# Attention as one stream of block steps over all head pairs, with the normalising on ScalarE

## The chip, the core and the metric

The kernel runs on one core of a Trainium2 chip. A core has TensorE (PE in the profile; its weight loads stand apart as PEld), VectorE (DVE), ScalarE (ACT), GpSimd (POOL), and SyncE (SP), which here only issues transfers. Each engine works through its own list of instructions in order. The metric is device microseconds of one execution.

## The reference

One inference step of a two-layer network on 640 tokens (512 latent, 128 context) of width 1024. Both layers are half FFN, mixer, half FFN. The mixer of layer 0 is a Fourier transform, that of layer 1 is attention, and only that attention is touched here. Cut to it:

```python
q, k, v = split(h @ w_qkv)                        # 16 heads of 64
# context queries (128): all context keys
p = softmax(q k^T);  o = p v
# latent queries (512 = 8 rows x 64 columns): 8 x 16 neighbours with a bias, and 128 cached keys
p = softmax(concat(q k_win^T + bias, q k_cache^T));  o = p_loc v_win + p_ctx v_cache
y = o @ w_out
```

## The kernel before

Activations lie transposed, channels on partitions and tokens along the row, in two halves of 320 tokens. Projections are made with split operands: each weight and each activation is a high part and a low part, and `mm3` (L206) makes one product of three matmuls (L209 to L211). Weights come as units of 128x1024. `send` (L166) loads a unit into one of four `raw` buffers, ScalarE writes its high part (L192) and VectorE its low part (L194) into one of six slots.

Attention (`attention`, L890) works by head pair: channel block c of eight holds heads 2c and 2c+1. `qk(c)` projects queries and keys of a pair, 96 matmuls, and writes them in two parts (L909 to L940); `double` (L950) copies the keys to the other 64 partitions. `v_tiles` projects values for two pairs at once, five token tiles of 24 matmuls each.

The attention of one pair is five blocks: four of 128 latent queries with 384 keys, and one, "c", for the context queries. A block has three pieces for each head. **Scores**: two matmuls into PSUM (L1041), VectorE adds the bias, writes `left` and takes the maximum (L1045), negates it (L1028), ScalarE takes the exponential and its sum (L1029), VectorE takes the reciprocal (L1030) and multiplies `left` by it (L1031). **Turn**: three transposes on TensorE (L1055), and ScalarE copies the result out of PSUM into `right` (L1057). **Values**: products with v, `right` as the moving operand, accumulated in the PSUM bank `sum` (L1070); the two heads write 64 PSUM partitions each. There are four `left` buffers, three `right` buffers, two `score` banks, and one each of `turn` and `sum`. In step n of a pair stand the scores of block n, the values of block n-2, and the turns of block n-1; after five steps two more empty the pipeline.

What sets the order: `weave` (L879) takes the list of a pair's pieces and a length in ns, and `tick` drops a piece into the projections each time that an assumed amount of matmul time has passed. So the pieces of pair c lie between the projections of pair c+1. `flush` emits what is left, and `behind` (L197) emits jobs of the next modulation: one job loads 128x1024 weights into a `raw` buffer and has VectorE make two dot products of them (L349). A scheduler then orders each engine's list by priority and readiness of its own; the pieces are what it is given, the list is what it makes.

Pairs 0 to 6 run under the projections of the next pair. Pair 7 runs under the first seven eighths of the first four output projections (`out_proj`, L749), whose input is `y`, split into two parts (L203, L204).

Of the kernel before, what the change touches and what calls it, by code (L numbers as in the profile page):

```python
# [15 lines left out]
ALU = mybir.AluOpType  # L16
PSUM = bass.MemoryType.PSUM

P = 128
# [50 lines left out]
for _c in range(2, NCH):  # L70
    QKV_ORDER += [("q", _c), ("k", _c)]
    if _c % 2 == 0 and _c > 2:
        QKV_ORDER += [("v0", _c // 2), ("v1", _c // 2)]
# [37 lines left out]
class Kernel:  # L111
# [778 lines left out]
    def attention(self, base, boundary):  # L890
# [70 lines left out]

        def v_tiles(quad, ts, at=at, bank="main"):
# [4 lines left out]
            for t in ts:  # L967
# [6 lines left out]
                for i, v in enumerate(values[quad]):  # L974
                    nc.vector.tensor_copy(v[:, t, :], ps[:, i * P : (i + 1) * P])
                    if t == 4:
                        nc.sync.dma_start(out=io["v_out"][2 * quad + i], in_=v[:, t, :])

        for half in (0, 1):
            self.finish(half)  # L980
            if half == 0:
                for c in (0, 1):
                    open_pair(c)
                    cached(c)
            pss = self.multi([self.unit(base + i) for i in range(4)], half)
            for i, ps in enumerate(pss):
                with self.tc.high_priority():
                    (query, key)[i % 2](i // 2, half, ps)
            if half:
                double(0)  # L990
                double(1)
            for quad in (1, 0) if half == 0 else (0,):
                while half == 0 and not self.normed[1][1 - quad]:
                    self.step(1)
                v_tiles(quad, ((0, 1), (2, 3, 4))[half], at if half else early, "score")
        qk_ns, v_ns = 4 * 8 * 3 * 147.0, 5 * 8 * 3 * 118.0
# [10 lines left out]
        parts = self.pair_parts(NCH - 1, pairs[NCH - 1], ctx_qk[NCH - 1], values[3][1])  # L1007
        for c in range(NCH - 1):
            for half in (0, 1):
                self.split(self.h.at(0, c, half), self.h.at(1, c, half), self.pair(self.y, c, half, 1))  # L1010
        self.weave(parts, 8000)
        def rest():
            self.flush()
            for half in (0, 1):
                self.split(self.h.at(0, NCH - 1, half), self.h.at(1, NCH - 1, half), self.pair(self.y, NCH - 1, half, 1))
        self.out_proj(1, base + len(QKV_ORDER), boundary, rest)

    def pair_parts(self, c, pair, qk, v):
# [3 lines left out]
        ks = pair[1:]  # L1022
        cache_v = self.cache[1][:, c * P : (c + 1) * P]
        state = {}

        def softmax(L, mx, w):
            sm = self.col(1)
            nc.vector.tensor_scalar_mul(mx, mx, -1.0)  # L1028
            nc.scalar.activation(L[:, :w], state["in"], AF.Exp, bias=mx, accum_out=sm)  # L1029
            nc.vector.reciprocal(sm, sm)  # L1030
            nc.vector.tensor_scalar_mul(L[:, :w], L[:, :w], sm)  # L1031

        def scores(p0, b):
# [5 lines left out]
            q = queries(pair, p0)[:, b * P : (b + 1) * P]  # L1039
            for part in range(2):  # L1040
                nc.tensor.matmul(o, q, tiles(ks[p0])[:, 5 * part : 5 * part + 5][:, BLOCK_KEYS[b]],  # L1041
                                 start=part == 0, stop=part == 1)
# [3 lines left out]
                                           scale=1.0, scalar=-3e38, op0=ALU.add, op1=ALU.max, accum_out=mx)  # L1046
            state["in"] = L
            softmax(L, mx, 384)
            state[p0, b] = L

        def turn(which, w):
            L = state.pop(which)
# [5 lines left out]
            state["t", which] = ptb  # L1058

        def values(b):  # L1060

            ptb = [state.pop(("t", (p0, b))) for p0 in range(2)]
# [3 lines left out]
            for at, q0, nq, tiles in taken:  # L1066
                for n, (i, k) in enumerate(tiles):
                    for p0 in range(2):
                        ds = slice(64 * p0, 64 * p0 + 64)
                        nc.tensor.matmul(state["o"][ds, q0 : q0 + nq], cache_v[:, ds] if k is None else v[:, k, ds],  # L1070
# [7 lines left out]
        def ctx_scores(p0):  # L1078
            ps = self.bank("score")
            nc.tensor.matmul(ps[:, :P], qk[:, p0 * P : (p0 + 1) * P], qk[:, 2 * P :], start=True, stop=True)  # L1080
            L = self.temp("left")
            mx = self.col(1)
            nc.vector.tensor_reduce(out=mx, in_=ps[:, :P], axis=mybir.AxisListType.X, op=ALU.max)
            state["in"] = ps[:, :P]
            softmax(L, mx, P)
            state[p0, "c"] = L

        blocks = [0, 1, 2, 3, "c"]
        both = lambda do: [partial(do, p0) for p0 in range(2)]
        parts = []  # L1090
        for n in range(len(blocks) + 2):
            if n < len(blocks):
                b = blocks[n]
# [150 lines left out]
```

## Time and profile before

| | us |
|---|---|
| median of three runs (2374.76 to 2378.6) | 2376.35 |
| the profiled execution | 2376.43 |
| its span, first to last instruction | 2374.6 |
| attention with its projections, 1571 to 1871 of the span | 300 |
| ... up to the first scores, to 1622 | 51 |
| ... pairs 0 to 5, to 1808 | 186 |
| ... pair 6, to 1844 | 36 |
| ... pair 7, to 1871 | 27 |

The borders are those of the copies that end a pair (L1076), rounded. In a profile, "PE sum L1070 <- ACT right L1057" means that the matmul of L1070 into `sum` stood idle until the ScalarE instruction of L1057 that wrote `right` had ended. TensorE is pipelined: the interval from one matmul's start to the next one's start is what a matmul costs, not its duration.

### The profile page before, as it was taken

Reading aid. Unit: us, or ns where it says so; the run is one execution under the profiler, and the core shown is the slowest. Engines: PE = TensorE matmul, PEld = TensorE weight load, DVE = VectorE, ACT = ScalarE, POOL = GpSimd, SP = SyncE. Lnnn points to the kernel's source line nnn. Section 1 sums busy time; section 2 is a strip of 40 time slices with the busy share of each in tenths; the row PEclk is TensorE's granted clock in tenths of the full one; section 3 lists DMA queues with packets and bytes.
Section 4 is the critical chain, followed back from the end, with each engine's and each line's share of the span. In section 5 each row is a group of like instructions: output and inputs, shape, how many; then the busy total and the mean of one; then the engine's idle time right before and its main releaser. Section 6 shows DMA issues by size and latency. Waiting matters only on the chain.

```text
span 2374.6 us, 39530 instructions
## 1 busy us (share of the span) xinstructions
PE 2302.0 (97%) x15692; PEld 2249.1 (95%) x15692; DVE 1743.5 (73%) x3112; ACT 1277.0 (54%) x2444; POOL 48.8 (2%) x50
## 2 busy tenths in 40 slices
PE   6899999998999999999999999999999999999997
PEld 5899999998999999999999999988888899999997
DVE  7788888389788878846878887368888585755553
ACT  3445545564564545547545555555556574545545
POOL 3200000000000000000000000000000000000000
PEclk9999999999999999999999999999999999999999
DMA  7134334333424433442234434223444222321241
GB/s 264 58 125 143 119 129 135 132 102 124 151 72 143 148 119 109 140 160 91 94 118 134 143 116 149 100 72 121 132 137 129 81 97 72 98 85 58 89 134 45
DMA packets 80142, 277.10 MB, mean 117 GB/s; under 512 B 8786, under 2 KB 15186, under 8 KB 79956
## 3 DMA queue, kind: packets, MB, share of 16 engines
q1 hardware_dynamic: 79684, 274.25, 35.5%
q8 instruction: 123, 2.02, 0.3%
q14 instruction: 63, 0.52, 0.1%
q10 hardware_dynamic: 272, 0.33, 0.0%
HBM read 263.00 MB, written 11.53 MB: 116 GB/s over the span
## 4 chain that ended last, share of the span: by engine, by line
PE 87%; DVE 5%; ACT 4%; issue 2%; DMA 1%; POOL 0%; SPq 0%; ACTq 0%; DVEq 0%
PE main L209 25%; PE main L211 25%; PE main L210 25%; PE score L209 2%; PE score L210 2%; PE score L211 2%; PE sum L1070 2%; DVE junk L349 1%; ACT hi L192 1%; PE turn L1055 1%; PE score L1041 1%; DVE lo L194 1%; PE sum L432 1%; DVE ring L204 1%; ACT right L1057 1%
## 5 line engine op out<-in xcount | busy, mean ns | idle before, releaser
L209 PE MATMUL main<-ring,hi 128*128 128x320 f32 x3872 | 1200.2, 311 | 19.5 <-ACT ring L203 18.1
L211 PE MATMUL main<-ring,lo 128*128 128x320 f32 x3872 | 1203.0, 311 | 2.9 <-POOL lo L194 2.9
L210 PE MATMUL main<-ring,hi 128*128 128x320 f32 x3872 | 1203.8, 311 | 1.6 <-DVE ring L204 1.5
L209 PEld LDWEIGHTS main<-ring,hi 128*128 128x128 f32 x3872 | 728.5, 188 | 25.5 <-ACT ring L203 20.3
L210 PEld LDWEIGHTS main<-ring,hi 128*128 128x128 f32 x3872 | 730.4, 189 | 5.2 <-DVE ring L204 3.1
L211 PEld LDWEIGHTS main<-ring,lo 128*128 128x128 f32 x3872 | 730.5, 189 | 5.0 <-POOL lo L194 3.4
L192 ACT ACTIVATE hi<-raw 128x1024 fp32r<-128x1024 f32 (+1 forms) x358 | 350.7, 982 | 480.9 <-PE main L210 385.4
L194 DVE TENSOR_TENSOR lo<-raw,hi 128x1024 fp32r<-128x1024 f32 (+1 forms) x354 | 398.3, 1125 | 167.9 <-ACT hi L192 166.7
L349 DVE SCALAR_TENSOR_TENSOR junk<-raw,wide 128x1024 bf16<-128x1024 f32 x256 | 312.4, 1220 | 12.8 <-DMA raw<-in_w_mod_t 10.1
L644 ACT ACTIVATE y<-main 128x320 f32<-128x320 f32 x320 | 138.3, 433 | 175.1 <-PE main L211 173.9
L385 DVE TENSOR_TENSOR total<-total,square 128x640 f32<-128x640 f32 x71 | 58.3, 823 | 115.8 <-ACT square L384 114.9
L632 ACT ACTIVATE main<-y 128x320 f32<-128x320 f32 x256 | 111.7, 439 | 23.5 <-DVE left L618 9.9
L210 PE MATMUL score<-ring,hi 128*128 128x320 f32 x384 | 118.7, 309 | 0.4 <-DVE ring L204 0.4
L209 PE MATMUL score<-ring,hi 128*128 128x320 f32 x384 | 118.9, 310 | 0.0
L211 PE MATMUL score<-ring,lo 128*128 128x320 f32 x384 | 118.6, 309 | 0.0
L194 DVE TENSOR_TENSOR lo<-sums,hi 128x1024 fp32r<-128x1024 f32 x64 | 78.2, 1222 | 54.0 <-ACT hi L192 54.0
L211 PE MATMUL main<-ring,ring 128*128 128x320 f32 x352 | 109.7, 312 | 5.8 <-POOL ring L194 5.8
L209 PE MATMUL main<-ring,ring 128*128 128x320 f32 x352 | 111.2, 317 | 0.0
L210 PE MATMUL main<-ring,ring 128*128 128x320 f32 x352 | 109.4, 311 | 0.0
L192 ACT ACTIVATE hi<-sums 128x1024 fp32r<-128x1024 f32 x64 | 67.9, 1060 | 27.3 <-PE main L210 20.5
L203 ACT ACTIVATE ring<-right 128x320 fp32r<-128x320 f32 x112 | 51.6, 469 | 45.6 <-DVE right L531 37.1
L604 DVE TENSOR_TENSOR left<-left,main 128x320 f32<-128x320 f32 x64 | 31.2, 487 | 59.6 <-PE main L211 59.6
(189 smaller groups left out, 2803.2 us busy)
## 6 DMA issues: line engine op xcount, KB each, us to landing
raw<-in_w SPq DMA_DIRECT2D x264, 512.0 KB, 3.6
raw<-in_w_mod_t SPq DMA_DIRECT2D x128, 512.0 KB, 3.7
raw<-in_qkv SPq DMA_DIRECT2D x26, 512.0 KB, 3.6
spill<-ring SPq DMA_DIRECT2D x12, 640.0 KB, 3.4
ring<-spill SPq DMA_DIRECT2D x12, 640.0 KB, 4.7
raw<-in_bias SPq DMA_DIRECT2D x16, 448.0 KB, 3.4
first<-in_w_mod_t SPq DMA_DIRECT2D x8, 512.0 KB, 10.2
raw<-in_four_in SPq DMA_DIRECT2D x8, 512.0 KB, 3.5
```

Of the source, the lines that this page charges most:

```text
L192: nc.scalar.activation(hi, raw[:, at], AF.Copy)
L194: engine.tensor_tensor(lo, raw[:, at], hi.bitcast(F32), op=ALU.subtract)
L203: self.nc.scalar.activation(hi, src, AF.Copy)
L209: mm(out, whi, xhi, start=start, stop=False)
L210: mm(out, whi, xlo, start=False, stop=False)
L211: self.latest = mm(out, wlo, xhi, start=False, stop=stop)
L349: last = self.nc.vector.scalar_tensor_tensor(out=self.junk, in0=raw, scalar=1.0, in1=self.wide[:, cond, :], op0=ALU.mult, op1=ALU.mult, ac ...
L385: nc.vector.tensor_tensor(acc, acc, sq, op=ALU.add)
L604: tt(a, q, z, op=ALU.subtract)
L632: nc.scalar.activation(ps[:, :HALF], self.y[:, m, lo:hi], AF.Copy)
L644: nc.scalar.activation(self.y[:, m, lo:hi], ps[:, :HALF], AF.Copy)
L1070: nc.tensor.matmul(state["o"][ds, q0 : q0 + nq], cache_v[:, ds] if k is None else v[:, k, ds], ptb[p0][:, i * P + at : i * P + at + nq], s ...
```

## The change

All forty blocks of the eight pairs become one list of steps (`attend` in place of `pair_parts`), so the pipeline is not emptied between pairs: step n holds the scores of block n, the values of block n-2 and the turns of block n-1 over the border of a pair. Five steps are woven into the projections of the next pair. The projections of values are spread over more pairs, two or three token tiles at a time; those of the second half of pair 1's queries and keys move behind the first scores. The multiplication by the reciprocal moves from VectorE to ScalarE (`scale`), ahead of the values of the block before. The negation of the maximum is folded into the scores' reduction (scale -1, minimum) and the exponential (scale -1); for "c" it stays. `behind` emits one modulation job in a step instead of three or four at the end of a pair. The split of `y` for pair 6 moves into the last steps.

```diff
-        for half in (0, 1):
-            self.finish(half)
...
-            pss = self.multi([self.unit(base + i) for i in range(4)], half)
...
-        for c in range(NCH - 1):
-            v_next = {0: 1, 3: 2, 5: 3}.get(c)
-            self.weave(self.pair_parts(c, pairs[c], ctx_qk[c], values[c // 2][c % 2]),
-                       (qk_ns if c else 0) + (v_ns if v_next else 0) - (0 if c else v_ns * 0.4))
-            if c:
-                qk(c + 1)
-            if v_next:
-                v_tiles(v_next, range(5) if c else (2, 3, 4))
-            self.flush()
-            self.behind(3 + (c < 3))
+        steps = self.attend(pairs, ctx_qk, values)
+        period = lambda c: [part for step in steps[5 * c : 5 * c + 5] for part in step]
+        qk_ns, v_ns = 4 * 8 * 3 * 147.0, 8 * 3 * 118.0
+        self.finish(0)
...
+        products([("q", 0), ("k", 0), ("q", 1), ("k", 1)], 0)
...
+        self.finish(1)
+        products([("q", 0), ("k", 0), ("v", 0, 3), ("v", 0, 4)], 1)
+        double(0)
+        v_tiles(0, (2,), early, "score")
+        plan = {0: (1, (2, 3, 4)), 2: (2, (0, 1)), 3: (2, (2, 3, 4)), 4: (3, (0, 1)), 5: (3, (2, 3, 4))}
+        for c in range(NCH - 1):
+            quad, ts = plan.get(c, (0, ()))
+            self.weave(period(c), (qk_ns if c else qk_ns / 2) + len(ts) * v_ns)
...
-        self.weave(parts, 8000)
+        steps[5 * NCH - 4].append(partial(parts_of, NCH - 2))
+        self.weave([part for step in steps[5 * NCH - 5 :] for part in step], 9000)
...
-            nc.vector.tensor_scalar_mul(mx, mx, -1.0)
-            nc.scalar.activation(L[:, :w], state["in"], AF.Exp, bias=mx, accum_out=sm)
+            nc.scalar.activation(L[:, :w], src, AF.Exp, bias=mx, scale=sign, accum_out=sm)
             nc.vector.reciprocal(sm, sm)
-            nc.vector.tensor_scalar_mul(L[:, :w], L[:, :w], sm)
...
+        def scale(c, b):
+            for p0 in range(2):
+                L, sm, w = state[c, b, p0]
+                nc.scalar.activation(L[:, :w], L[:, :w], AF.Copy, scale=sm)
...
+        blocks = [(c, b) for c in range(NCH) for b in (0, 1, 2, 3, "c")]
+        steps = []
         for n in range(len(blocks) + 2):
+            parts = []
             if n < len(blocks):
-                b = blocks[n]
-                parts += both(ctx_scores if b == "c" else lambda p0, b=b: scores(p0, b))
-            if n >= 2:
-                parts.append(partial(values, blocks[n - 2]))
-            if 1 <= n <= len(blocks):
-                b = blocks[n - 1]
-                parts += both(lambda p0, b=b: turn((p0, b), P if b == "c" else 384))
-        return parts
+                c, b = blocks[n]
+                parts += [partial(ctx_scores if b == "c" else scores, c, b, p0) for p0 in range(2)]
+            before = partial(scale, *blocks[n - 1]) if 1 <= n <= len(blocks) else None
+            after = partial(take, *blocks[n - 2]) if n >= 2 else None
+            parts.append(lambda both=(before, after): [do() for do in both if do])
+            if before:
+                parts += [partial(turn, *blocks[n - 1], p0) for p0 in range(2)]
+            if n < 35 and (n % 5 < 3 or n in (3, 8, 13)):
+                parts.append(self.behind)
+            steps.append(parts)
```

How the lists move. First place: TensorE in pair 6, block steps. `score`, `turn` and `sum` are PSUM banks, `main` rows are projections. Before, from a score on:

```order
L1041 MATMUL score_18967<-ring_18381,ring_18379 128x384 x2
L1055 MATMUL turn_18981<-ident,left_18923 128x128 x3
L210 MATMUL main_19000<-ring_15818,hi_18521 128x320
L211 MATMUL main_19000<-ring_15817,lo_18522 128x320
L209 MATMUL main_19098<-ring_15737,hi_18653 128x320
L210 MATMUL main_19098<-ring_15738,hi_18653 128x320
L211 MATMUL main_19098<-ring_15737,lo_18654 128x320
L1070 MATMUL sum_19035<-right_18985,square_18649 64x64
L209 MATMUL main_19098<-ring_15737,hi_18653 128x320
```

and in the change, from the turn of a block's second head on (the row after the last is the first of the six values that use this turn):

```order
L1103 MATMUL turn_19046<-ident,left_18933 128x128 x3
L209 MATMUL main_19016<-ring_15792,hi_18551 128x320
L210 MATMUL main_19016<-ring_15793,hi_18551 128x320
L211 MATMUL main_19016<-ring_15792,lo_18552 128x320
L1077 MATMUL score_19066<-ring_18543,ring_18542 128x384 x2
L209 MATMUL main_19016<-ring_15817,hi_18551 128x320
L210 MATMUL main_19016<-ring_15818,hi_18551 128x320
L211 MATMUL main_19016<-ring_15817,lo_18552 128x320
L1077 MATMUL score_19078<-ring_18544,ring_18542 128x384 x2
L209 MATMUL main_19016<-ring_15817,hi_18551 128x320
L210 MATMUL main_19016<-ring_15818,hi_18551 128x320
L211 MATMUL main_19016<-ring_15817,lo_18552 128x320
```

Before, one value matmul follows the turn that feeds it after five projections, alone, and the other rows of its block come later as a second group; in the change nine projections and two scores lie between, and the values of a block stand together. From the first score to the last value, TensorE's list enters a group of values 79 times before (41 of these groups are one row) and 55 times in the change (15 of one row); the number of rows is the same, 224.

Second place: TensorE at the end of pair 7. Before, 39 rows of scores, turns and values follow the last projection of the stretch, among them:

```order
L1055 MATMUL turn_19490<-ident,left_19407 128x128 x3
L1080 MATMUL score_19508<-rms_19083 128x128
L1080 MATMUL score_19521<-rms_19083 128x128
L1055 MATMUL turn_19499<-ident,left_19418 128x128 x3
L1070 MATMUL sum_19429<-right_19494,ring_15811 64x128
L1070 MATMUL sum_19429<-right_19503,ring_15811 64x128
```

In the change projections reach in between the two turns of the last latent block:

```order
L1103 MATMUL turn_19480<-ident,left_19404 128x128 x3
L209 MATMUL main_19259<-ring_15817,hi_19012 128x320
L210 MATMUL main_19259<-ring_15818,hi_19012 128x320
L211 MATMUL main_19259<-ring_15817,lo_19013 128x320
L209 MATMUL main_19282<-ring_15817,hi_19220 128x320
L210 MATMUL main_19282<-ring_15818,hi_19220 128x320
L211 MATMUL main_19282<-ring_15817,lo_19221 128x320
L1103 MATMUL turn_19489<-ident,left_19416 128x128 x3
L1119 MATMUL sum_19374<-right_19484,square_18261 64x128
```

From the turn of the second head on, eleven rows of turns and values stay behind the last projection.

Third place: ScalarE in the change, while the blocks of pair 4 run. `hi` is the high part of a weight unit, `ring` from `main` the high part of keys:

```order
L192 ACTIVATE hi_18264<-raw_18262 128x1024
L1105 ACTIVATE right_18128<-turn_18124 128x384
L1097 ACTIVATE left_18071<-left_18071,col_18074 128x384
L1063 ACTIVATE left_18146,col_18149<-left_18146,col_18147 128x384
L936 ACTIVATE ring_17955<-main_18117 64x128
L936 ACTIVATE ring_17956<-main_18117 64x128
L936 ACTIVATE ring_17955<-main_18117 64x192
L936 ACTIVATE ring_17956<-main_18117 64x192
L1063 ACTIVATE left_18161,col_18164<-left_18161,col_18162 128x384
L192 ACTIVATE hi_18270<-raw_18268 128x1024
L1105 ACTIVATE right_18200<-turn_18196 128x384
L1097 ACTIVATE left_18146<-left_18146,col_18149 128x384
```

The scaling (L1097) of a block is a new row in this list, between exponentials (L1063), copies of turns (L1105) and splits. Outside the attention the lists of all engines are the same as before, row for row.

More of the change, by code (lines that the diff above doesn't have):

```diff
@@ L71 @@
     QKV_ORDER += [("q", _c), ("k", _c)]
-    if _c % 2 == 0 and _c > 2:
-        QKV_ORDER += [("v0", _c // 2), ("v1", _c // 2)]
+    if _c in (3, 5):
+        QKV_ORDER += [("v0", _c // 2 + 1), ("v1", _c // 2 + 1)]
 QKV = list(dict.fromkeys(QKV_ORDER))
@@ L1001, in attention @@
             if c:
                 qk(c + 1)
-            if v_next:
-                v_tiles(v_next, range(5) if c else (2, 3, 4))
+            else:
+                for which, put in (("q", query), ("k", key)):
+                    ps = self.proj(self.unit(early[which, 1]), lambda kk: kk * P, 1)
+                    with self.tc.high_priority():
+                        put(1, 1, ps)
+                double(1)
+            if ts and c not in (3, 5):
+                v_tiles(quad, ts)
             self.flush()
-            self.behind(3 + (c < 3))
```

122 lines of the change are left out of this document (70 added, 52 removed).

## Prediction

> **What bounds the kernel now.** First the page: TensorE is busy nearly throughout, and the chain that ended last runs over it.
>
> ```profile
> span 2374.6 us, 39530 instructions
> PE 2302.0 (97%) x15692; PEld 2249.1 (95%) x15692; DVE 1743.5 (73%) x3112; ACT 1277.0 (54%) x2444; POOL 48.8 (2%) x50
> PE 87%; DVE 5%; ACT 4%; issue 2%; DMA 1%; POOL 0%; SPq 0%; ACTq 0%; DVEq 0%
> ```
>
> These are averages. The change stays in the attention, so next the busy times of its stretches: up to the first scores, pairs 0 to 5, pair 6, pair 7 (columns: length, then PE, PEld, DVE, ACT, POOL, the granted clock, DMA).
>
> ```profile
> 1571.00:1622.00 51.00, 46.14 (x345) 45.53 (x343) 35.81 (x82) 24.71 (x57) 0.41 (x2) 0.97 0.20 63
> 1622.00:1808.00 186.00, 181.25 (x1346) 157.20 (x1344) 160.76 (x507) 103.31 (x287) 10.05 (x24) 1.00 0.42 132
> 1808.00:1844.00 36.00, 32.45 (x217) 26.79 (x215) 29.34 (x94) 23.28 (x62) 0.00 (x0) 0.95 0.41 130
> 1844.00:1871.00 27.00, 24.31 (x176) 20.00 (x175) 20.98 (x67) 13.70 (x36) 0.00 (x0) 1.00 0.44 137
> ```
>
> TensorE is idle for 4.86 + 4.75 + 3.55 + 2.69 = 15.9 us of 300. VectorE is at 160.76/186 = 86% in the middle; ScalarE has room. Third, what TensorE waits for there (total us, times, longest):
>
> ```profile
> PEld sum L1070 <- ACT right L1057: 19.9, 54, 1.2
> PE sum L1070 <- ACT right L1057: 6.5, 14, 1.0
> ...
> PE main L210 <- DVE lo L194: 0.6, 1, 0.6
> PE score L209 <- DVE total L975: 0.6, 1, 0.6
> ```
>
> The value products come too soon after the copy of their turn; in the first row it is their weight loads that wait, in the second the matmuls. So the stage is bound by TensorE, plus what its order costs.
>
> **The price of the order.** A piece of TensorE's timeline in pair 1:
>
> ```profile
> 1662.03 0.31 PE L209 MATMUL main<-ring,hi 128*128 128x320 f32 x1
> 1662.27 0.19 PEld L1070 LDWEIGHTS sum<-right,total 128*64 128x64 f32 x2 [0.19 <-ACT right L1057]
> 1662.27 0.43 PE L1070 MATMUL sum<-right,total 128*64 128x128 f32 x2
> ...
> 1662.63 0.42 PE L210 MATMUL main<-ring,hi 128*128 128x320 f32 x1
> 1662.88 0.31 PE L211 MATMUL main<-ring,lo 128*128 128x320 f32 x1
> 1663.03 0.31 PE L209 MATMUL main<-ring,hi 128*128 128x320 f32 x1
> 1663.18 0.51 PE L1041 MATMUL score<-ring,ring 128*128 128x384 f32 x2
> 1663.53 0.49 PE L1055 MATMUL turn<-ident,left 128*128 128x128 f32 x3
> 1663.77 0.39 PE L210 MATMUL main<-ring,hi 128*128 128x320 f32 x1
> 1664.01 0.30 PE L211 MATMUL main<-ring,lo 128*128 128x320 f32 x1
> ...
> 1664.44 0.30 PE L211 MATMUL main<-ring,lo 128*128 128x320 f32 x1
> ...
> 1665.47 0.42 PE L209 MATMUL main<-ring,hi 128*128 128x320 f32 x1
> 1665.73 0.33 PE L1041 MATMUL score<-ring,ring 128*128 128x384 f32 x1
> ```
>
> Undisturbed, a projection takes 0.15 us from start to start (1662.88 to 1663.03), two scores 0.35, three turns 0.33 (1663.53 to 1664.01 less one projection). A lone value row (two instructions in a trace) takes, from the projection before it to the second after it, 0.85 us less two projections = 0.56. The other five rows of its block (1664.44 to 1665.73, again less two) take 1.00. So a row costs (1.00 - 0.56)/4 = 0.11 and entering and leaving a group 0.45; turns and scores have no such price.
>
> **The change, part by part.**
>
> (1) *Groups of values, 79 to 55.* 24 entries at 0.45 are 10.8 us. If the 0.19 that the timeline names as waiting belongs to the neighbourhood of the turn and not to the entry, the entry is 0.26: 6.2 us. I take **-8**, nearer to the wait's side of the middle, since a wait that goes is counted in (2).
>
> The Trainium skill, page "TensorEngine Tiling (Array Packing)", section "Tiling Modes", says that changing the tiling mode drains TensorE; values write 64 PSUM partitions each and everything else 128. By it the 0.45 are all entry, and the term would be -10.8; the row cannot part the two.
>
> (2) *Waits in pairs 0 to 5.* Nine projections and two scores, 9 x 0.15 + 2 x 0.35 = 2.0 us, now part the turn from its values, and the copy takes 0.49 (row below). Of the 4.75 us idle I keep 1.5: **-3.2**; ends 0 and -4.75, and what the weight loads' row holds beyond is in (1).
>
> (3) *Pair 6.* Idle 3.55, and after three waits in a row TensorE lost its clock:
>
> ```profile
> 1838.00:1840.00 2.00, 1.61 (x7) 1.14 (x9) 2.00 (x10) 1.07 (x4) 0.00 (x0) 0.53 0.00 0
> 1840.00:1842.00 2.00, 2.00 (x14) 1.67 (x15) 1.19 (x6) 0.47 (x3) 0.00 (x0) 0.61 0.73 222
> ```
>
> At 0.53 and 0.61 that is 2 x 0.47 + 2 x 0.39 = 1.7 us of clock. VectorE was busy all of the first window; it loses the scaling and the negations. **-3.5** of 5.25; ends 0 and -5.25.
>
> (4) *Pair 7.* The last projection, and the next one after the attention:
>
> ```profile
> 1857.28 0.31 PE L211 MATMUL main<-ring,lo 128*128 128x320 f32 x1
> 1858.08 0.27 PE L1070 MATMUL sum<-right,square 128*64 128x64 f32 x1 [0.49 <-ACT right L1057]
> ...
> 1870.55 0.85 PE L209 MATMUL main<-ring,hi 128*128 128x320 f32 x4
> ```
>
> 12.5 us without a projection, for 27 value rows (3.0 us), six threes of turns and two single ones (2.2), two scores and two of context (about 1.0): 6.2 us of work, 6.3 of waits and entries. In the change eleven rows stay bare: 3 + 8 x 0.11 and two waits for copies, about 0.7 each with the way there and back (estimate from 0.49 and 0.28 for the copies), two entries: 3.5 us, of which 2 are lost. So up to 4.3 comes back; less the entries of (1), **-3**; ends 0 and -4.3.
>
> (5) *Entry.* The lo-split and the copy that cost 0.6 each are now behind other projections. But the first score comes 29 projections and 24 value matmuls after the last product of the first two, 29 x 0.15 + 24 x 0.12 (an estimate from 256 columns against 320) = 7.2 us, and VectorE has to write the low parts of q and k, three lo-splits and the first doubling by then:
>
> ```profile
> L194 DVE TENSOR_TENSOR lo<-raw,hi 128x1024 fp32r<-128x1024 f32 x26 | 31.6, 1218 | 12.3 <-ACT hi L192 12.2
> L950 DVE CAST ring<-ring 64x1280 fp32r<-64x1280 f32 x16 | 13.2, 822 | 0.5
> ```
>
> 3 x 1.22 + 0.82 = 4.5, and some 13 small ones at an estimated 0.3: 8.4, behind a high part of 1 us on ScalarE: 2 us late. **+0.7**; ends -1.2 and +3.
>
> (6) *Scaling on ScalarE.* Out of VectorE go 26.9 + 4.5 (sixteen at 0.28, an estimate by width) + 64 x 0.146 = 40.7 us. Into ScalarE come 80 instructions with a scale from a column; that form stands in the trace for other widths:
>
> ```profile
> L1031 DVE TENSOR_SCALAR left<-left,col 128x384 f32<-128x384 f32 x64 | 26.9, 421 | 0.3
> L1028 DVE TENSOR_SCALAR col<-col 128x1 f32<-128x1 f32 x80 | 11.7, 146 | 0.4
> L405 ACT ACTIVATE y<-y,coef 128x320 f32<-128x320 f32 x48 | 24.4, 557 | 0.8
> L405 ACT ACTIVATE y<-y,coef 128x128 f32<-128x128 f32 x48 | 18.8, 391 | 0.0
> L1029 ACT ACTIVATE left<-left,col 128x384 f32<-128x384 f32 x64 | 39.2, 612 | 29.3 <-DVE col L1028 29.0
> L1057 ACT ACTIVATE right<-turn 128x384 f32<-128x384 f32 x64 | 31.4, 490 | 37.3 <-PE turn L1055 36.6
> ```
>
> 391 to 557 ns over 192 columns gives 613 at 384: 64 x 0.613 + 16 x 0.391 = 45.5 us, on 140.3 of 249 (the last three stretches): 186, or 79% of some 235. VectorE falls from 211 to 170. What hides it is ScalarE's idle time; without that cover it is up to +45. Per step (249/40 = 6.2 us) the chain score 0.35, reduction about 0.6, exponential with its sum 0.8, reciprocal 0.16, scaling 0.61 is 2.5, and the second head's exponential and scaling 1.4 more, so the turn a step later finds its input unless splits or dot products stand between. **+1.5**; ends 0 and +12 (a rival).
>
> The Trainium skill, page "ScalarE: Activation LUTs", section "Rules for kernel authors", says to multiply on VectorE rather than on ScalarE. Here the multiplication does cost more there, 613 against 421; by the rule the term would be 64 x 0.19 = +12 if engine time were what counts, which holds only where ScalarE sets the pace.
>
> (7) *Modulation jobs one at a time.* The same 24, each two dot products and one load on SP into the same four buffers; a unit or bias load may now stand behind one. VectorE's room hides the 2.4 us of a job; bare it is up to 24 x 2.4. I cost it at 0 beside (6).
>
> Sum: -8 - 3.2 - 3.5 - 3 + 0.7 + 1.5 = **-15.5** on a span of 2374.6; with the 1.8 around it (2376.43, the median being 2376.35) **2361 us**.
>
> **The rivals.**
>
> *A. All waits go.* (1) at 10.8, (2) to (4) at their ends 4.75 + 5.25 + 4.3, entry -1.2: -26, **2350**. For it: two of three named waits lose their cause. Against it: each engine keeps its in-order list.
>
> *B. The dot products take the waits' place.* A job's 2 x 1.22 us stands between a reduction and a reciprocal, the scaling is late, the turn waits in half of 24 steps by 1 us: +12 for (6), a sum of -5.0, **2371**. For it: VectorE stays at 73%. Against it: 6.2 us of step for a chain of 4.
>
> *C. ScalarE sets the pace: slower.* It must fit 186/40 = 4.65 us into each step, so it decides from 1.55 us of waits per step on. Its waits now:
>
> ```profile
> ACT right L1057 <- PE turn L1055: 48.8, 48, 2.3
> ACT left L1029 <- DVE col L1028: 33.9, 30, 6.4
> ```
>
> 82.7/40 = 2.1 per step. If half of the first stays, all of the second and 0.5 for the reciprocals: 4.65 + 0.6 + 0.85 + 0.5 = 6.6, 0.4 x 40 = +16, with (1) at -8: **2384**. Against it: the waits for turns are waits for TensorE, and shrink as ScalarE falls behind.
>
> **How the numbers follow.** Forecast 0.58, A 0.17, B 0.15, C 0.10. The forecast's own range is 2354 to 2368. The range, 2348 to 2376, takes in A and B. What this kernel's measurement can tell is about 0.2%, 4.75 us: faster means under 2371.6. The forecast and A are faster, and B, at 2371, falls on both sides, 0.06 and 0.09: faster 0.58 + 0.17 + 0.06 = 0.81; same 0.09 from B and 0.01 from C; slower 0.09.
>
> **What would show it.** Right: the attention about 285 us long, values waiting for `right` under 2 us, no lost clock in pair 6, pair 7 without a bare stretch of 12 us. (6) is wrong if turns wait for `left`; C is right if ScalarE's idle time is gone and projections or turns wait for it. The whole is wrong if the entry of a group of values costs the same per row however it is cut.

## The result and the profile after

The change takes 2360.3 us (median of four, 2358.29 to 2361.94), the kernel before 2376.07 on the same chip: a ratio of 0.9932, with a 95% interval of 0.9915 to 0.9949. The forecast was 2361. The profiled execution took 2358.87 us. Its page has these lines for those shown of before:

```profile
span 2357.0 us, 39382 instructions
PE 2291.1 (97%) x15692; PEld 2244.9 (95%) x15692; DVE 1718.2 (73%) x2968; ACT 1313.8 (56%) x2524; POOL 46.7 (2%) x50
PE 86%; DVE 5%; ACT 4%; DMA 2%; issue 2%; POOL 0%; SPq 0%; ACTq 0%; DVEq 0%
```

TensorE makes the same 15692 matmuls. The span is 17.6 us shorter, and all of it lies in the attention: from 1571 to the first projection behind it are 299.6 us before and 282.1 now. The stretches of the change up to the first score, to the end of pair 5, of pair 6 and of pair 7 (columns: length, then PE, PEld, DVE, ACT, POOL, the granted clock, DMA share and GB/s):

```profile
1571.00:1611.00 40.00, 35.55 (x262) 34.95 (x261) 27.66 (x61) 21.54 (x50) 0.40 (x2) 0.96 0.16 45
1611.00:1808.00 197.00, 192.20 (x1475) 172.03 (x1476) 162.20 (x449) 141.35 (x366) 9.06 (x24) 1.00 0.46 147
1808.00:1836.00 28.00, 27.15 (x209) 24.05 (x208) 22.67 (x72) 26.31 (x72) 0.00 (x0) 1.00 0.33 104
1836.00:1854.00 18.00, 17.35 (x132) 13.54 (x130) 7.71 (x26) 13.61 (x36) 0.00 (x0) 1.00 0.41 129
```

Projections moved over the borders of pairs, so the lengths are not compared one by one. Two things can be read: the clock in pair 6 is 1.00, where it was 0.95, and ScalarE is busy for 26.31 of 28 us there. TensorE is idle for 10.8 us of 283 in the four rows, where it was 15.9 of 300. What its matmuls and its weight loads wait for in the attention of the change (total us, times, longest):

```profile
ACT right L1105 <- PE turn L1103: 22.1, 32, 2.7
...
PEld turn L1103 <- ACT right L1105: 10.3, 23, 1.1
...
PE turn L1103 <- ACT right L1105: 4.5, 11, 0.8
...
PEld turn L1103 <- ACT left L1097: 1.3, 3, 0.7
...
PEld sum L1119 <- ACT right L1105: 1.1, 3, 0.5
...
PE turn L1103 <- ACT left L1097: 0.5, 1, 0.5
PE sum L1119 <- ACT right L1105: 0.2, 1, 0.2
```

Values wait for `right` no more: 6.5 us of matmuls and 19.9 of weight loads have become 0.2 and 1.1. In their place turns wait, 4.5 and 10.3 us, where before these were the rows:

```profile
PEld turn L1055 <- ACT right L1057: 3.4, 7, 0.9
...
PE turn L1055 <- ACT right L1057: 1.6, 4, 0.6
```

A turn that waits for a copy into `right` waits for the *previous* turn: there is one `turn` bank, and it comes free when ScalarE has copied it. The forecast looked for turns that wait for the scaled `left`; those rows have 0.5 us at matmuls and 1.3 at weight loads.

What a group of values costs can be read more closely now, since lone rows stand between projections with no wait named at all. TensorE's timeline of the change, first a lone row, then a whole block of six rows (12 records) among projections of 256 columns:

```profile
1670.61 0.31 PE L211 MATMUL main<-ring,lo 128*128 128x320 f32 x1
1670.84 0.43 PE L1119 MATMUL sum<-right,total 128*64 128x128 f32 x2
1671.21 0.42 PE L209 MATMUL main<-ring,hi 128*128 128x320 f32 x1
1671.46 0.31 PE L210 MATMUL main<-ring,hi 128*128 128x320 f32 x1
...
1684.98 0.28 PE L211 MATMUL main<-hi,ring 128*128 128x256 f32 x1
1685.19 0.44 PE L1119 MATMUL sum<-right,square 128*64 128x128 f32 x4
...
1685.99 0.39 PE L209 MATMUL main<-hi,ring 128*128 128x256 f32 x1
1686.22 0.28 PE L210 MATMUL main<-lo,ring 128*128 128x256 f32 x1
```

The lone row takes 0.85 us less two projections of 0.147, so 0.56: the same as where 0.19 of it was called a wait. The six rows take 1.24 less two of 0.12, so 1.00, and that is also what the prediction read for five rows. Groups of four records take 0.56 too (four of four in the change, 0.560 to 0.569), groups of eight 0.78 in the run with values cut, groups of ten 0.99 to 1.00 (five of seven in the run with the scaling on VectorE), and of 28, below, 1.87. So two and four records cost the same, and so do ten and twelve: rows count by twos, one for each head. In the five rows of before that the prediction read, the first rows of the two heads start 0.01 us apart, so the heads run beside each other:

```profile
1664.67 0.32 PE L1070 MATMUL sum<-right,total 128*64 128x128 f32 x1
1664.68 0.32 PE L1070 MATMUL sum<-right,ring 128*64 128x128 f32 x1
```

A group costs 0.34 us and 0.22 for each two rows of 128 queries; a row without its partner in the group, an odd row, takes the 0.22 alone, 0.11 more than its share of two. The rows of block 0 hold 64 queries; a lone one takes 0.46 and eight take 0.81, so two of them cost 0.12 and an odd one is 0.06 dearer. With that, the groups' own price, beside rows that all stand in twos, is 79 x 0.34 + 52 x 0.11 + 16 x 0.06 = 33.5 us before and 55 x 0.34 + 24 x 0.11 + 4 x 0.06 = 21.6 in the change.

### The profile page after: what moved, and what is told of

The parts are those of the page before. It is cut to its first block, busy times and chain, and to the rows that moved or that the text cites. A ratio compares the mean times of both kernels' runs of the same rounds, so it can differ in the third digit from the quotient of the medians.

```text
span 2357.0 us, 39382 instructions
## 1 busy us (share of the span) xinstructions
PE 2291.1 (97%) x15692; PEld 2244.9 (95%) x15692; DVE 1718.2 (73%) x2968; ACT 1313.8 (56%) x2524; POOL 46.7 (2%) x50
## 4 chain that ended last, share of the span: by engine, by line
PE 86%; DVE 5%; ACT 4%; DMA 2%; issue 2%; POOL 0%; SPq 0%; ACTq 0%; DVEq 0%
PE main L209 25%; PE main L211 25%; PE main L210 25%; PE score L209 2%; PE score L210 2%; PE score L211 2%; DVE junk L349 2%; ACT hi L192 1%; PE sum L1119 1%; PE turn L1103 1%; PE score L1077 1%; DVE lo L194 1%; PE sum L424 1%; DMA raw<-in_w 1%; PE sum L432 1%
```

## The experiments

All times are medians of several runs beside runs of the kernel before on the same chip. "Groups' price" is worked out as just said, from the odd rows of 128 queries and those of 64; "attention" is the length from 1571 of the span to the first projection behind the last value, in the profiled execution.

| kernel | groups, lone ones; odd rows | groups' price, us | attention, us | time, us | ratio to before, 95% |
|---|---|---|---|---|---|
| before | 79, 41; 52 + 16 | 33.5 | 299.6 | 2376 | 1 |
| the change | 55, 15; 24 + 4 | 21.6 | 282.1 | 2360.3 | 0.9915 to 0.9949 |
| second head first | 44, 0; 0 + 2 | 15.1 | 280.3 | 2356.7 | 0.9900 to 0.9927 |
| ... and three banks | 40, 0; 0 | 13.6 | 269.7 | 2346.7 | 0.9854 to 0.9884 |
| ... and blocks together | 20, 0; 0 | 6.8 | 266.3 | 2345.6 | 0.9853 to 0.9880 |
| values cut | 77, 19; 24 + 4 | 29.1 | 289.5 | 2366.3 | 0.9938 to 0.9963 |
| scaling on VectorE | 62, 22; 34 + 8 | 25.3 | 288.1 | 2365.8 | 0.9940 to 0.9968 |
| before, scaled on ScalarE | 66, 29; 38 + 12 | 27.3 | 291.6 | 2368.7 | 0.9947 to 0.9972 |
| jobs in bursts | 49, 8; 10 + 8 | 18.2 | 283.0 | 2359.2 | 0.9915 to 0.9940 |
| pairs emptied | 63, 27; 34 + 10 | 25.8 | 290.5 | 2367.8 | 0.9952 to 0.9977 |
| three banks, values full width | 39, - | 0 | 264.7 | 2341.8 | 0.9838 to 0.9868 |
| blocks together, keys first | 19, 0; 0 | 6.5 | 271.2 | 2347.4 | 0.9860 to 0.9893 |
| three banks, keys first | 41, 0; 0 | 13.9 | 267.8 | 2344.6 | 0.9852 to 0.9881 |
| ... and scaling shared | 40, 0; 0 | 13.6 | 269.6 | 2346.8 | 0.9852 to 0.9885 |

### Is the price of a group real, and what is it?

**Second head first.** A scheduler lets the first head's matmul go as soon as that head's copy is there, and the rest of the block comes later: that is where lone rows come from. In this run the head whose copy comes last stands first.

```diff
-                    for p0 in range(2):
+                    for p0 in (1, 0):
                         ds = slice(64 * p0, 64 * p0 + 64)
```

> The changed kernel, with one thing different: in the values of a block the matmul of the second head stands ahead of that of the first, so that a group cannot begin before both copies of the turns are there. TensorE's list then enters a group of values 44 times instead of 55; the work is the same, and 40 is the least with one group per block. If each entry costs 0.45 us whatever the group holds (the forecast's theory): 11 x 0.45 = 5.0 us less than the change's 2360.3, so 2355.3. If what the forecast called the entry was a wait for the copies, which has fallen from 6.5 to 0.2 us of idle already, there is nothing left to gain: 2360, with the waits for right at 0.2 us or above.

2356.7 us, 3.6 less than the change. The price fell by 6.5, and part of it came back as waits: matmuls of values for `right` 1.4 us (0.2), turns for `left` 1.6 (0.5). Wait theory would have had nothing.

**Values cut.** The opposite: 22 groups more.

```diff
-            after = partial(take, *blocks[n - 2]) if n >= 2 else None
+            after = partial(take, *blocks[n - 2], (0,)) if n >= 2 else None
...
+            if n >= 2 and blocks[n - 2][1] != "c":
+                parts.append(partial(take, *blocks[n - 2], (1, 2, 3)))
```

> The changed kernel, with the values of each latent block given out as two pieces, the first row of both heads and the rest, and pieces of other work between them; all have their copies by then or have them later than now. 77 groups instead of 55. Entry theory: 22 x 0.45 = 9.9 us more than 2360.3, so 2370.2, with idle time for right still below 1 us. Wait theory: no more than now, 2360, since the waits for right cannot grow by it.

2366.3, 6.0 us more, and 7.4 more in the attention of the profile; the groups' price rose by 7.5. Matmuls of values wait 0.4 us for `right`. So a group costs what it costs without a wait, and the prediction's 0.45 was too high for a group as such: it holds 0.34 for the group and 0.11 because its lone row has no partner.

**Values in full width.** On the kernel with three banks (below). The matmuls write all 128 PSUM partitions; only the second head's are made.

```diff
-                    for p0 in (1, 0):
-                        ds = slice(64 * p0, 64 * p0 + 64)
+                    for p0 in (1,):
+                        ds = slice(0, 128)
```

> As the run with three common banks, but values are taken for the second head only, with the v of both heads as weights, so that each matmul writes 128 PSUM partitions instead of 64 (left out: the product of the first head's probabilities; its scores, turn and copy are still made). 112 matmuls instead of 224, in 39 groups. If the price of entering a group (0.34 us, 13.6 us over 40 groups) belongs to the change between matmuls that write 64 partitions and those that write 128, it is gone: a group costs only its rows, as the turns do, and the time is 2346.7 - 13.6 = 2333 if two rows of 64 partitions cost as much as one of 128. If the price belongs to leaving the projections at all, for a PSUM bank of its own or for plain f32 operands, it stays: 2346.7, and a group of three rows costs 0.34 more than its rows. Rows that cost less or more than two of the others would shift both by the same amount; the prices of groups of three and of four rows tell that.

TensorE's timeline of this run, a block of three rows between projections of 320 columns:

```profile
1711.49 0.31 PE L211 MATMUL main<-ring,lo 128*128 128x320 f32 x1
1711.64 0.38 PE L1119 MATMUL sum<-right,square 128*128 128x128 f32 x2
1711.86 0.39 PE L1119 MATMUL sum<-right,ring 128*128 128x128 f32 x2
1712.08 0.39 PE L1119 MATMUL sum<-right,square 128*128 128x128 f32 x2
1712.22 0.39 PE L209 MATMUL main<-ring,hi 128*128 128x320 f32 x1
1712.45 0.30 PE L210 MATMUL main<-ring,hi 128*128 128x320 f32 x1
```

0.96 us less two projections is 0.67, and rows stand 0.22 apart, so three rows cost three rows. A group of one row costs 0.22, one of four 0.89. The price of entering is gone, with the same operands, the same PSUM bank and the same neighbours. It belongs to the change between matmuls that write 64 partitions and those that write 128. The Trainium skill, page "TensorEngine Tiling (Array Packing)", section "Tiling Modes", says that a change of the tiling mode drains TensorE. This trace agrees in that there is a price, 0.34 us for the way in and out; that it is a drain the trace does not show.

The time is 2341.8, only 4.9 us below the 2346.7 of its base, not the 13.6 expected. Of that difference 3.6 is arithmetic: block 0 has four rows per head over 64 queries each, which cost 0.89 in full width against 0.81 as a group of 64 partitions, so the groups' own cost falls by 24 x 0.33 + 8 x 0.34 - 8 x 0.08 = 10.0. The other 5 us are not accounted for row by row; the waits of turns for what the exponential writes into `left` grew, at matmuls from 0.6 to 2.4 us.

### What the turns wait for

**Three banks.** With the second head first, turns and scores share three PSUM banks.

```diff
-BANKS = {"main": 4, "score": 2, "turn": 1, "sum": 1}
+BANKS = {"main": 4, "score": 3, "sum": 1}
...
-            pt = self.bank("turn")
+            pt = self.bank("score")
```

> As the run with the second head first, and turns and scores take turns in three common PSUM banks instead of two and one (the few other users of the one bank take the bank of sums). A turn then no longer has to wait until the turn just before it is copied. 40 groups of values. Entry theory: 15 x 0.45 = 6.8 us, and of the 4.5 us that turns wait for the copy of the turn before, between none and all: 2349.0 to 2353.5. Wait theory: only the 4.5, so 2355.8 to 2360; the waits of turns for right should be near 0 in both.

2346.7, below the lower end of what was expected, and 10.0 under the run with the second head first alone. In that run the turns waited for the copy of the turn before as in the change:

```profile
PEld turn L1103 <- ACT right L1105: 10.9, 24, 1.2
...
PE turn L1103 <- ACT right L1105: 4.9, 10, 1.0
```

and with three banks (a turn is now "score L1103"):

```profile
PE score L1103 <- ACT left L1097: 1.8, 3, 0.9
...
PEld score L1103 <- ACT right L1105: 1.4, 5, 0.6
...
PE score L1103 <- ACT right L1105: 0.3, 1, 0.3
```

15.8 us of waits became 1.7. The attention is 10.6 us shorter: 1.5 by the groups; 2.7 by its entry, where the first score stands at 1609.7 instead of 1612.4 and a wait of 2.7 us in the statistics ahead of it is gone and one of 1.9 for a weight's low part has come; the remaining 6.4 fit the turns. So this wait seems to have cost more than the 4.5 us at matmuls that the expectation allowed for: by this remainder, part of what stands at the weight loads is lost as well.

**Scaling on VectorE.** Was it the scaling on ScalarE that made the copies late?

```diff
-                nc.scalar.activation(L[:, :w], L[:, :w], AF.Copy, scale=sm)
+                nc.vector.tensor_scalar_mul(L[:, :w], L[:, :w], sm)
```

> The changed kernel with the multiplication by the reciprocal back on VectorE, at the same place in the program. 62 groups of values instead of 55, 22 of them one row instead of 15: by the prices that the first four runs gave (0.34 us per group, 0.11 more for a lone row) +3.2 us. Theory one, the scaling on ScalarE makes the copies of turns late and the turns wait 6 us for them: these waits go, 2360.3 + 3.2 - 6 = 2357.5. Theory two, the relief of VectorE was worth having (the forecast's terms 2 and 3): VectorE is back at 86%, half to all of 3.2 + 3.5 us of waits return, 2367 to 2370.

2365.8, 5.5 us more than the change; 3.7 of that are groups. And the turns still wait for copies, 11.3 us in all where it was 14.8:

```profile
PEld turn L1103 <- ACT right L1105: 8.9, 20, 1.1
...
PE turn L1103 <- ACT right L1105: 2.4, 5, 0.8
```

So theory one falls as the whole cause: the turns wait too where ScalarE is busy for 36 us less (1277.8 of the span instead of 1313.8). A copy ends, at the median, 0.80 us after the start of the last transpose in the change and 0.86 here and before; it is not late as a rule, though the slowest tenth takes 2.0 us or more in the change and 1.7 here. That one bank is too few for turns that follow one another closely is what the run with three banks shows. Theory two came nearer, though 1.8 us beside the groups are less than its 3.4 to 6.7.

**Before, scaled on ScalarE.** That part alone, with the folded negation.

```diff
-            nc.vector.tensor_scalar_mul(mx, mx, -1.0)
-            nc.scalar.activation(L[:, :w], state["in"], AF.Exp, bias=mx, accum_out=sm)
+            nc.scalar.activation(L[:, :w], state["in"], AF.Exp, bias=mx, scale=state["sign"], accum_out=sm)
             nc.vector.reciprocal(sm, sm)
-            nc.vector.tensor_scalar_mul(L[:, :w], L[:, :w], sm)
+            nc.scalar.activation(L[:, :w], L[:, :w], AF.Copy, scale=sm)
```

> The kernel before, with only the multiplication by the reciprocal moved to ScalarE (right behind the reciprocal) and the negation folded into reduction and exponential; pairs are still emptied one by one, values parted as before, modulation jobs in bursts. 66 groups instead of 79, 29 of one row instead of 42: -5.8 us by the prices of the first runs. Theory one (turns wait 6 us for late copies): 2376.1 - 5.8 + 6 = 2376. Theory two (VectorE's relief takes the waits of pairs 0 to 6 away): 2376.1 - 5.8 - 6.7 = 2363.6.

2368.7, 7.5 us under before and between the two theories. The groups' price falls by 6.2, so beside it 1.3 us are won; two of the five executions took 2364.9, so this remainder is not a sure one. Weight loads of values for `right` wait 6.0 us where it was 19.9. Turns wait longer than the 3.4 and 1.6 us of before:

```profile
PEld turn L1054 <- ACT right L1056: 7.6, 14, 1.1
...
PE turn L1054 <- ACT right L1056: 4.3, 9, 0.9
```

So the wait changes its place here already, without the stream: 11.9 us with the scaling alone, 11.3 with the rest of the change alone, 14.8 with both, 5.0 before.

### The other parts of the change

**Jobs in bursts.**

```diff
-            if n < 35 and (n % 5 < 3 or n in (3, 8, 13)):
-                parts.append(self.behind)
...
             self.flush()
+            self.behind(3 + (c < 3))
```

> The changed kernel with the 24 modulation jobs emitted in bursts of three or four at the end of a pair, as before. 49 groups instead of 55, 8 of one row instead of 15. The forecast has the jobs at nothing (term 7): only the groups count, 2360.3 - 2.8 = 2357.5. Rival: a burst of 7 to 10 us of dot products holds VectorE's reductions and reciprocals at a pair's end, one wait of 0.5 to 1 us in each of seven: 2361 to 2364.5.

2359.2 (2358.8 to 2361.35): 1.1 us under the change, which cannot be told from nothing. One job at a time was worth nothing that can be measured; it may have cost the six groups.

**Pairs emptied.** The steps are made pair by pair, and with them the split of `y` for pair 6 stands ahead of pair 7 again; the rest is as in the change.

```diff
-        blocks = [(c, b) for c in range(NCH) for b in (0, 1, 2, 3, "c")]
         steps = []
-        for n in range(len(blocks) + 2):
-            parts = []
+        for c in range(NCH):
+            blocks = [(c, b) for b in (0, 1, 2, 3, "c")]
+            for n in range(len(blocks) + 2):
+                parts = []
```

> The changed kernel without the stream: the steps of each pair are closed by two steps without scores, as before, and the next pair begins anew; scaling, parting of the projections and single modulation jobs stay. 63 groups instead of 55, 27 of one row instead of 15: +4.0 us. If the stream was worth only this: 2364.3. If emptying the pipeline also costs two waits for a copy (about 0.7 us each) at each of seven pair ends, up to 10 us more: 2374.

2367.8, 7.5 us more: 4.2 by the groups, and 3.3 that are left for waits, a third of the 10 that the second reading allowed.

### How far it goes

**Blocks together.** Values of two or three blocks in one group of up to 28 records.

```diff
-        blocks = [(c, b) for c in range(NCH) for b in (0, 1, 2, 3, "c")]
+        order = (0, 1, "c", 2, 3)
+        blocks = [(c, b) for c in range(NCH) for b in (order if c < NCH - 1 else (0, 1, 2, 3, "c"))]
...
+                due = [(c, b)] if c >= NCH - 1 else {1: [(c, 0), (c, 1)], 3: [(c, "c"), (c, 2), (c, 3)]}.get(b, [])
...
-            ptb = self.temp("right")
-            nc.scalar.activation(ptb[:, :w], pt[:, :w], AF.Copy)
+            nc.scalar.activation(L[:, :w], pt[:, :w], AF.Copy)
```

> As the run with three common banks, and for pairs 0 to 6 the values of two or three blocks are taken in one go: blocks 0 and 1 together, and blocks c, 2 and 3 together (the order of a pair is 0, 1, c, 2, 3; the copy of a turn goes back into the buffer that it came from, seven such buffers in place of four and three). 20 groups of values instead of 55, the same 224 rows. Entry theory: 35 x 0.45 = 15.8 us, and between 0 and 4.5 from the turns' waits: 2340.0 to 2344.5. Wait theory: 2355.8 to 2360 again, since the number of groups is no cost; a burst of 14 rows without a projection would cost nothing in either.

TensorE's timeline of this run shows such a group at the price worked out above, 2.11 us from the projection before it to the second after it, less two of 0.12, 1.87 (28 records are seven twos of rows, 0.34 + 7 x 0.22 = 1.88):

```profile
1693.11 0.28 PE L211 MATMUL main<-hi,ring 128*128 128x256 f32 x1
1693.31 0.44 PE L1119 MATMUL sum<-left,square 128*64 128x128 f32 x4
...
1694.99 0.39 PE L209 MATMUL main<-hi,ring 128*128 128x256 f32 x1
1695.22 0.28 PE L210 MATMUL main<-lo,ring 128*128 128x256 f32 x1
```

Yet 2345.6 us is 1.1 under the run with three banks (3.4 in the attention), where 6.8 had gone from the groups' price. New waits took it back, the doubled keys first (4.7 where it was 2.3) and the context blocks, whose probabilities lie in the `rms` buffers here:

```profile
PE score L1077 <- DVE ring L950: 4.7, 4, 1.6
...
PEld score L1103 <- ACT rms L1063: 2.9, 3, 1.1
...
PE score L1103 <- ACT rms L1063: 2.1, 3, 0.8
```

**Keys first.** The edit, in two kernels: with blocks together, and with single blocks and three banks.

```diff
-            for which, put in (("q", query), ("k", key)):
+            for which, put in (("k", key), ("q", query)):
                 for half in (0, 1):
...
-            double(c)
+                if which == "k":
+                    double(c)
...
-        double(0)
+        with self.tc.high_priority():
+            double(0)
```

> As the run with blocks taken together, with two edits for the wait that was the longest there (scores waiting 4.7 us, four times, for the doubled keys): keys are projected ahead of queries from pair 2 on, so that the doubling runs under the queries' projection, and the first doubling has priority. 19 groups of values. If that wait goes: 2345.6 - 3.5 - 0.3 = 2342. If the queries' low parts, which VectorE now writes last, take its place: 2345, with scores waiting for what the queries' split writes.

> As the run with three common banks and single blocks, with the same two edits (keys first, the first doubling with priority). 41 groups of values. Waits for the doubled keys were 2.3 us there, two of them: 2346.7 - 1.2 = 2345.5 if one of the two goes. Against the run with blocks together and keys first it has 22 groups more: 22 x 0.34 = 7.5 us longer than that by the entry theory, if nothing else differs; less, if the blocks taken together have waits of their own, as the first pair of such runs suggests (6.8 by the groups, 1.1 measured).

With blocks together 2347.4, a miss. The wait for doubled keys is no longer among the long ones, but scores now wait for a turn's copy (L1111), which gives one of the three common banks back, and for the low parts of the queries (L924):

```profile
PEld score L1084 <- ACT left L1111: 6.6, 6, 2.6
...
PE score L1084 <- ACT left L1111: 2.7, 2, 2.4
PE score L1084 <- DVE ring L924: 2.4, 2, 2.1
```

With single blocks 2344.6 (2343.1 to 2347.2): the fastest median of the complete kernels, but not to be told from 2345.6, 2346.7 or the next. It has 22 groups more than the run just named, 7.4 us by their price, and is not the slower one: here the blocks taken together lose in waits of their own all that they save in groups.

**Scaling shared.** On that kernel, the second head scaled by VectorE.

```diff
-                nc.scalar.activation(L[:, :w], L[:, :w], AF.Copy, scale=sm)
+                if p0:
+                    nc.vector.tensor_scalar_mul(L[:, :w], L[:, :w], sm)
+                else:
+                    nc.scalar.activation(L[:, :w], L[:, :w], AF.Copy, scale=sm)
```

> As the run with single blocks and keys first, and the multiplication by the reciprocal is shared out: that of the first head on ScalarE, that of the second on VectorE. 40 groups of values instead of 41. In that run turns and scores waited 2.7 us (weight loads) and 1.4 us (matmuls) for what the scaling on ScalarE writes. If ScalarE's list is what is late there: 2344.6 - 3 = 2341.6, and these two rows shrink to under half. If VectorE is as short of time as ScalarE (it gets 32 x 0.42 + 8 x 0.28 = 15.7 us back, and with all of the scaling on VectorE the change lost 2.3 us beyond its groups): 2344.6 to 2346.

2346.8 (2343.7 to 2349.6), nothing won. Turns still wait, now for VectorE's half of the scaling, and values wait for their copies:

```profile
PEld sum L1129 <- ACT right L1115: 5.3, 11, 1.0
...
PEld score L1113 <- DVE left L1105: 2.0, 4, 0.9
```

Five versions end at 2344.6 to 2347.4 us, 13 to 16 us below the change, with 41 groups or with 19. What holds these was not settled; waits that went in one run stood at another instruction in the next.

## Why the prediction was right, and where it was not

The time (2361 against 2360.3) and the signs that it named came as foreseen: the attention 282.1 us long ("about 285"), values waiting for `right` 0.2 + 1.1 us ("under 2"), the clock of pair 6 kept, and no bare stretch of 12 us. Term by term:

- **(1) Groups, -8.** The groups' price fell by some 12 us, beyond the upper end, 10.8. The 0.19 us that a row of the timeline called waiting is no wait: lone rows without it cost the same 0.56. What was misread is the step from five rows at 1.00 and one at 0.56 to 0.11 for a row: five rows take as long as six, and one as long as two. So the entry is 0.34, not 0.45, and a row without its partner, which the term put at nothing, costs 0.11 more (0.06 in block 0). The 24 entries give 8.2, near the -8 by luck, since that was a middle between 0.45 and 0.26; 40 odd rows fewer give another 3.8.
- **(2) Waits in pairs 0 to 5, -3.2.** The wait that it named went, as argued, but TensorE's idle time in that stretch is 4.80 us where it was 4.75. What the forecast missed is that a wait of the same kind arose at the turns: there is one bank for them. Neither the scaling nor the stream is its only cause, as the two runs with one of them each show (11.9 and 11.3 us); three banks take it away, and about 6.4 us with it.
- **(3) Pair 6, -3.5.** Right in kind: clock 1.00, idle 0.85 us of 28 instead of 3.55 of 36. The 1.7 us of clock and 2.7 of idle make 4.4, as far as stretches of different length can be compared. That it is VectorE's relief that did it is not shown: the clock stays at 0.99 or above there also with the scaling on VectorE, with pairs emptied, and in the kernel before with the scaling on ScalarE.
- **(4) Pair 7, -3.** Right in what stays bare. The bare stretch, in TensorE's timeline of the change:

```profile
1849.43 0.49 PE L1103 MATMUL turn<-ident,left 128*128 128x128 f32 x3
...
1850.50 0.32 PE L1119 MATMUL sum<-right,square 128*64 128x128 f32 x1 [0.22 <-ACT right L1105]
...
1852.00 0.33 PE L1103 MATMUL turn<-ident,left 128*128 128x128 f32 x1 [0.37 <-ACT right L1105]
...
1853.06 0.85 PE L209 MATMUL main<-ring,hi 128*128 128x320 f32 x4
```

3.6 us where 3.5 were worked out, with two waits for copies, smaller than the 0.7 set for each.

- **(5) Entry, +0.7.** The first scores wait 1.1 us for the doubled keys, where 2 were foreseen, at the place that was named. That the entry as a whole has more to give showed only with three banks.
- **(6) Scaling on ScalarE, +1.5.** The durations were right, 609 and 397 ns against 613 and 391, in the groups of the change:

```profile
L1097 ACT ACTIVATE left<-left,col 128x384 f32<-128x384 f32 x64 | 38.2, 609 | 5.0 <-DVE col L1064 4.5
...
L1097 ACT ACTIVATE left<-left,col 128x128 f32<-128x128 f32 x16 | 6.2, 397 | 4.4 <-DVE col L1064 2.9 <-DVE col L1091 1.6
```

The sign of the term was not. Taken back, the scaling costs 5.5 us, 1.8 of them beside the groups; alone, with the folded negation, it wins 7.5 on the kernel before. The step that failed is that only the harm on ScalarE was priced there; that the scheduler puts the values closer together with it, 13 groups fewer by this part alone, was counted under (1) for the change as a whole, and why it does so was not traced. The Trainium skill's rule (page "ScalarE: Activation LUTs", section "Rules for kernel authors") to multiply on VectorE would have cost 5.5 us here. Engine time was not what counted: VectorE takes 421 ns for it and ScalarE 609, but VectorE was the fuller engine, 86% against 56% in pairs 0 to 5 of before.
- **(7) Jobs, 0.** Nothing that can be measured.

The rest beside the groups, as the forecast had it: -3.2 - 3.5 - 3 + 0.7 + 1.5 = -7.5. Measured: the span's 17.6 less 12, so -5.6. Inside it stands a new wait of several us at the turns that the forecast did not have; the trace does not part the other gains further. So the total fits better than its parts: the groups gave 4 us more than was set and the rest 2 less, and the median lies 1.4 above the profiled execution. That the time was hit within 1 us is therefore partly luck.

Rival A (2350) did not come because not all waits went: TensorE is still idle for 10.8 us, and turns wait for their bank. The run with the second head first and three banks gets there and beyond. B (2371) and C (2384) do not show: turns wait 0.5 us for `left` (1.3 at weight loads), and ScalarE has 80 us of its 283 idle.

## What to carry to other kernels

Count how often an engine's list changes between forms that do not go together, not only the instructions: here each way in and out was 0.34 us with nothing waiting, rows were cheap only in twos, and the cheapest way to fewer groups was to put the operand that comes last first in its group. A wait that has been removed should be looked for one stage earlier, at every buffer of which there is only one; moving work to the idler engine can pay even where it takes longer there. And when several edits that each remove a proven cost end at the same time, the cost has moved on, and the next edit has to begin from a new list of waits.

## What was not expected of the hardware

- Two value matmuls of 64 partitions, one for each head, start 0.01 us apart and take 0.22 us between them, as long as one of 128 partitions. So the two heads run beside each other for nothing but the price of entering, 0.34 us. A matmul without its partner takes the 0.22 alone: groups of two and of four records both cost 0.56 us, groups of ten and of twelve 1.00.
- A wait that the profile shows at weight loads seems neither free nor a loss in full: with three banks 15.8 us of waits for the bank (10.9 of them at weight loads) became 1.7, and about 6.4 us of time came back, as what is left beside groups and entry.
